# Background work on VectorE pinned in emission order, with larger costs per step, in a hybrid mLSTM and sparse attention block

## The chip, the cores and the metric

The kernel runs on one core of a Trainium2 chip. The metric is the device time of one execution in microseconds (us); three runs give the time of the kernel before, and one more execution was recorded by the hardware profiler.

## What is computed

A decoder block over 512 tokens of width 1024, in float32. One input projection feeds two groups of heads: an mLSTM with four heads behind a short causal convolution, and an attention with eight heads in which each token keeps the 128 best keys by an indexer's score. Both are gated, one output projection joins them, and a gated per-layer embedding and a final norm follow. Cut to what matters here:

```python
def block(x, p, ...):
    u = rmsnorm(x, norm_in)
    m_q, m_k, m_v, m_o, m_z, m_if, a_q, a_k, a_v, a_z, ix_q, ix_k, ix_w = split(u @ w_in)
    mq, mk = split(silu(causal_dwconv(concat(m_q, m_k), conv_w)))      # four taps
    log_i, log_f = m_if[:, :4] + b, log_sigmoid(m_if[:, 4:] + b)
    hm = sigmoid(m_o) * rmsnorm(mlstm(mq, mk, m_v, log_i, log_f)) * m_norm * silu(m_z)
    score = sum_h ix_w[h] * relu(ix_q[h] @ ix_k.T)                      # causal
    sel = top_k(score, 128)
    ha = softmax(a_q @ a_k.T / 8 + rel_bias, over sel) @ a_v * silu(a_z)
    h = x + concat(hm, ha) @ w_out
    h = h + (p @ w_ple) * sigmoid(h @ w_ple_gate)
    return rmsnorm(h, norm_final)
```

## The kernel before

Tokens are cut into four blocks of 128, channels into tiles of 128. Each operand of a product is split into a high and a low part (wh and wl for weights, uH and uL for the normed input), and each product is three matmuls (L212 to L214, or L232 to L234). Weights come in pieces of 128 x 1024; ScalarE rounds a piece to wh (L148), and wl = raw - wh is computed on GpSimd for the even pieces from 8 to 34 and on VectorE for the others (both L149).

TensorE runs the products one after the other: the indexer's queries, mq, mk (with the score matmuls is_ps, L506, put between them), mv in two passes of four PSUM banks, then the gates o and z, the mLSTM woven with further gates, av and aqk, the attention woven with aqk, az and the first output products, the output projection wo, and the embedding. The four banks of a dense product come free when its evacuation is done: for mk two copies on ScalarE (L462, L463), for mv a copy on ScalarE (L545, high part) and a subtraction on VectorE (L546, low part), for each of four token blocks. The evacuations carry a high priority. The score matmuls and the small products of the mLSTM use four other PSUM banks in turn.

Work that no product needs at once is background work: generators in the list `back`, `scores()` (relu on ScalarE, L509, and a weighted sum on VectorE, L514), `sequences()` (the gate scans, L479 to L494), eight `conv()` (three taps on VectorE, L450, a Tanh on ScalarE, L452, and a final step on VectorE, L453), and `topk()` (48 rounds, each a MAX, L524, and a MATCH_REPLACE, L525); later `split_mix()` (L595, L596) is added. `beat()` is called once in each group of dense matmuls and gives one unit of credit; it takes steps of the first generator while the credit isn't negative, and each step's cost (COST_SC, COST_CV, COST_TK, COST_MX, line 33) is taken off. This decides where the instructions are emitted. The final order of each engine's queue is set by a tile scheduler behind that, which moves an instruction ahead or back by its own view of readiness and priority unless it is pinned: `tc.keep_in_program_order` places an instruction behind the one traced just before it on its engine. Queues are in order: an instruction that waits holds all behind it. The bias table of the attention is loaded by a DMA that ScalarE's queue issues (`load_bias`, L440), and it waits for the write of `tdram` (L436).

Of the kernel before, what the change touches and what calls it, by code (L numbers as in the profile page):

```python
# [14 lines left out]
AF = mybir.ActivationFunctionType  # L15
OP = mybir.AluOpType
# [4 lines left out]
S = 512  # L21
# [8 lines left out]
DPLE = 256  # L30
EPS = 1e-6
NTMP, NKEEP = 8, 37
COST_SC, COST_CV, COST_TK, COST_MX, RATE = 1.3, 1.5, 1.5, 3.0, 1.4
NR, NW, ND, NS = 3, 4, 4, 1
QK0 = 10
POOLP = range(8, 36, 2)
# [11 lines left out]
def block_kernel(ctx: ExitStack, tc: tile.TileContext, x, p, w_in, b_gate, conv_w, w_out, norm_in,  # L48
                 m_norm, rel_bias, w_ple, w_ple_gate, norm_final, buckets, out):
    nc = tc.nc  # L50
    V, A, G, T = nc.vector, nc.scalar, nc.gpsimd, nc.tensor
# [30 lines left out]
    def col(name, n=1, bufs=1):  # L82
        return cp.tile([P, n], F32, tag=name, bufs=bufs, name=name)
# [30 lines left out]
    def cw(j, c):  # L114
        return vcols[:, 16 + 8 * j + c:17 + 8 * j + c]
# [52 lines left out]
        return ready.pop(k)  # L168

    back, credit = [], [0.0]  # L170

    def beat():

        credit[0] += 1.0
        while back and credit[0] >= 0.0:
            cost = next(back[0], None)
            if cost is None:
                back.pop(0)
            else:
                credit[0] -= cost  # L180
        if not back:
            credit[0] = 0.0
# [264 lines left out]
    def conv(c, raw):  # L447
        y = mqk[c]
        for j in range(1, 4):
            V.scalar_tensor_tensor(y[:, j:], raw[:, 0:S - j], cw(3 - j, c), y[:, j:], op0=OP.mult, op1=OP.add)  # L450
        yield COST_CV
        A.activation(raw, y, AF.Tanh, scale=0.5)  # L452
        V.scalar_tensor_tensor(y, raw, 1.0, y, op0=OP.add, op1=OP.mult)  # L453
        yield COST_CV

    def evac_qk(c0):
        def go(b, ps):
            c = c0 + b
            y = mqk[c] = keep(f"mqk{c}")
            raw = keep(f"raw{c}")  # L460
            with urgent():
                A.activation(raw, ps, AF.Copy)  # L462
                A.activation(y, ps, AF.Copy, scale=cw(3, c))  # L463
            back.insert(len(back) - 1, conv(c, raw))
        return go
# [3 lines left out]
    fr = [r[96:108, :] for r in rw]  # L469
    lr = [r[64:76, :] for r in rw]  # L470
# [5 lines left out]
    def sequences():  # L476
        A.activation(fr[1], fr[0], AF.Abs)
        A.activation(fr[2], fr[1], AF.Exp, scale=-1.0)
        A.activation(fr[1], fr[2], AF.Ln, bias=1.0)  # L479
        yield 1.0  # L480
        V.scalar_tensor_tensor(lr[2], fr[0], 0.0, fr[1], op0=OP.min, op1=OP.subtract)
        V.tensor_tensor_scan(lr[1], lr[2], lr[0], 0.0, op0=OP.add, op1=OP.max)
        yield 1.0

        arow = sp.tile([P, SW], F32, tag="sL", bufs=1, name="arow")
        ar = arow[64:76]
        for j in range(NT):
            n = S - j * P
            seg = ar[:, OFF[j]:OFF[j] + n]
            V.tensor_tensor_scan(seg, ones[64:76, :].to_broadcast([12, n]), lr[2][:, j * P:], 0.0, op0=OP.mult, op1=OP.add)  # L490
            V.tensor_tensor(lr[3][:, j * P:(j + 1) * P], lr[0][:, j * P:(j + 1) * P], seg[:, 0:P], OP.subtract)
            V.tensor_tensor(seg, seg, lr[1][:, j * P:], OP.subtract)
            yield 1.0
        nc.scalar.dma_start(adram, arow[72:76, 0:1280])  # L494


    sel, ended = {}, [False]
# [22 lines left out]
    def topk():  # L520
        for r in range(TOPK // 8):
            for i in range(1, NT):
                m8 = col(f"m8_{i}", 8, bufs=2)
                V.max(out=m8, in_=sel[i])  # L524
                V.match_replace(out=sel[i], in_to_replace=m8, in_values=sel[i], imm_value=-3e38)  # L525
                yield COST_TK
        for i in range(1, NT):
            V.tensor_scalar(sel[i], sel[i], -2e38, BIG, op0=OP.is_gt, op1=OP.mult)
        ended[0] = True

    back += [scores(), sequences(), topk()]
    run(dense_fm(4, evac_qk(0), name="mq"), dense_fm(4, evac_qk(4), name="mk"))

# [446 lines left out]
```

## Time and profile before

| | us |
|---|---|
| Time, median of three runs | 525.41 (525.35 to 527.21) |
| Profiled execution | 526.94 |
| its span | 524.9 |
| TensorE busy in the span | 498.6 |
| VectorE busy | 349.3 |
| ScalarE busy | 259.8 |
| GpSimd busy | 81.3 |

The span is the recorded stretch of the profiled execution, and all times of rows are counted from its start. A group of instructions is named by its line in the kernel, the engine, and the tiles that it writes and reads. A number in square brackets at the end of a timeline's row is the idle time of the engine ahead of it and what ended that. In the trace, mk runs until 96, pass 0 of mv from 98 to 121, pass 1 from 128 to 152, the first gates until about 198, the mLSTM's stage until about 313 and the attention's until about 400.

### The profile page before, as it was taken

The numbers are of one execution on the slowest core, as the hardware profiler recorded it, in microseconds if no ns is written. First come the engines' busy times: TensorE is split into PE (matmuls) and PEld (weight loads), VectorE is DVE, ScalarE is ACT, GpSimd is POOL, SyncE is SP. The second block draws the span as 40 slices with busy tenths as digits, with TensorE's granted clock in tenths as the row PEclk, the third lists the DMA queues.
The fourth block names the chain that finished last, engine by engine and source line by source line (L and its number), as shares of the span: only waits on it lengthen the run. The fifth ranks groups of instructions, "written<-read, shape, count | busy, mean of one in ns | idle before, by whom it ended". The sixth has DMA issues, their size and how long they took to land.

```text
span 524.9 us, 6706 instructions
## 1 busy us (share of the span) xinstructions
PE 498.6 (95%) x2370; PEld 409.3 (78%) x2370; DVE 349.3 (67%) x718; ACT 259.8 (49%) x518; POOL 81.3 (15%) x110
## 2 busy tenths in 40 slices
PE   4999999894999999999999999999999999999994
PEld 3887878683878888888888787888878888888884
DVE  0945287999999827355745759979887441452744
ACT  5636183763132425465545658767875321232533
POOL 4501022231111322310101012111111000000011
PEclk9999999997999999999999999999999999999998
DMA  8352557322223224223422312121123443213012
GB/s 264 108 181 84 104 87 172 117 82 81 81 85 116 82 81 140 77 92 112 131 81 90 102 61 76 46 81 74 47 82 121 161 160 113 88 41 120 1 51 109
DMA packets 37280, 52.24 MB, mean 100 GB/s; under 512 B 4156, under 2 KB 16732, under 8 KB 37248
## 3 DMA queue, kind: packets, MB, share of 16 engines
q1 hardware_dynamic: 30464, 42.34, 25.2%
q10 hardware_dynamic: 6688, 9.46, 7.3%
q8 instruction: 18, 0.29, 0.2%
q14 instruction: 14, 0.11, 0.1%
q0 software_dynamic: 96, 0.02, 0.0%
HBM read 48.13 MB, written 3.69 MB: 99 GB/s over the span
## 4 chain that ended last, share of the span: by engine, by line
PE 74%; DVE 12%; DMA 8%; ACT 2%; issue 2%; SPq 0%; POOL 0%; POOLq 0%; ACTq 0%; DVEq 0%
DMA tdram<-tv 7%; PE wo L233 4%; PE wo L232 4%; PE wo L234 4%; PE o L212 3%; PE z L212 3%; PE z L214 3%; PE o L213 3%; PE z L213 3%; PE o L214 3%; DVE mqk L450 2%; PE aqk L212 2%; PE aqk L213 2%; PE aqk L214 2%; PE mv L232 2%
## 5 line engine op out<-in xcount | busy, mean ns | idle before, releaser
L148 ACT ACTIVATE wh<-raw 128x1024 fp32r<-128x1024 f32 x70 | 74.0, 1058 | 110.6 <-PE wo L234 36.5
L149 DVE TENSOR_TENSOR wl<-raw,wh 128x1024 fp32r<-128x1024 f32 x56 | 68.6, 1225 | 68.5 <-ACT wh L148 68.3
L149 POOL TENSOR_TENSOR wl<-raw,wh 128x1024 fp32r<-128x1024 f32 x14 | 33.8, 2415 | 134.8 <-ACT wh L148 123.4
L232 PE MATMUL wo<-wh,mixH 128*128 128x512 f32 x96 | 38.9, 405 | 0.1
L234 PE MATMUL wo<-wh,mixL 128*128 128x512 f32 x96 | 37.9, 395 | 0.0
L233 PE MATMUL wo<-wl,mixH 128*128 128x512 f32 x96 | 37.9, 395 | 0.0
L232 PE MATMUL mv<-wh,uH 128*128 128x512 f32 x64 | 26.2, 410 | 8.5 <-DVE v L546 6.6
L212 PE MATMUL aqk<-uH,wh 128*128 128x512 f32 x64 | 26.4, 413 | 0.0
L234 PE MATMUL mv<-wh,uL 128*128 128x512 f32 x64 | 26.0, 406 | 0.0
L525 DVE MATCH_REPLACE8 sc<-m,sc 128x256 f32<-128x256 f32 (+2 forms) x48 | 25.8, 544 | 0.0
L212 PE MATMUL o<-uH,wh 128*128 128x512 f32 x64 | 25.8, 402 | 0.0
L212 PE MATMUL z<-uH,wh 128*128 128x512 f32 x64 | 25.7, 402 | 0.0
L233 PE MATMUL mv<-wl,uH 128*128 128x512 f32 x64 | 25.7, 401 | 0.0
L214 PE MATMUL aqk<-uH,wl 128*128 128x512 f32 x64 | 25.4, 397 | 0.0
L214 PE MATMUL z<-uH,wl 128*128 128x512 f32 x64 | 25.4, 396 | 0.0
L213 PE MATMUL o<-uL,wh 128*128 128x512 f32 x64 | 25.4, 396 | 0.0
L214 PE MATMUL o<-uH,wl 128*128 128x512 f32 x64 | 25.3, 396 | 0.0
L213 PE MATMUL z<-uL,wh 128*128 128x512 f32 x64 | 25.3, 396 | 0.0
L213 PE MATMUL aqk<-uL,wh 128*128 128x512 f32 x64 | 25.3, 395 | 0.0
L524 DVE MAX8 m<-sc 128x8 f32<-128x256 f32 (+2 forms) x48 | 24.8, 550 | 0.2 <-POOL sc L516 0.2
L731 POOL TENSOR_SCALAR bm<-sc,tz 128x128 f32<-128x128 f32 (+1 forms) x16 | 13.7, 857 | 71.3 <-DVE ha L772 21.2
L514 DVE SCALAR_TENSOR_TENSOR sc<-relu,iwt,sc 128x256 f32<-128x256 f32 (+2 forms) x21 | 14.2, 676 | 13.7 <-ACT relu L509 12.9
(245 smaller groups left out, 1363.6 us busy)
## 6 DMA issues: line engine op xcount, KB each, us to landing
raw<-in_w_in_dram SPq DMA_DIRECT2D x44, 512.0 KB, 3.4
raw<-in_w_out_dram SPq DMA_DIRECT2D x12, 512.0 KB, 3.5
raw<-in_w_in_dram SPq DMA_DIRECT2D x16, 256.0 KB, 2.9
raw<-in_w_ple_gate_dram SPq DMA_DIRECT2D x8, 512.0 KB, 3.5
x<-in_x_dram SPq DMA_DIRECT2D x8, 256.0 KB, 5.7
xr<-in_x_dram ACTq DMA_DIRECT2D x2, 1024.0 KB, 5.6
tdram<-tv ACTq DMA_DIRECT2D x1, 1536.0 KB
tz<-tdram ACTq DMA_DIRECT2D x1, 1024.0 KB, 6.3
```

The source lines that it names most:

```text
L148: A.activation(h, raw, AF.Copy)
L149: (G if k in POOLP else V).tensor_tensor(l, raw, f(h), OP.subtract)
L212: T.matmul(banks[b][:, 0:nt], h[:, k, bs], uH[:, kt, tok0:], start=(kt == 0), stop=False)
L213: T.matmul(banks[b][:, 0:nt], h[:, k, bs], uL[:, kt, tok0:], start=False, stop=False)
L214: T.matmul(banks[b][:, 0:nt], l[:, k, bs], uH[:, kt, tok0:], start=False, stop=(kt == KT - 1))
L232: T.matmul(banks[i], aH(kt, i), h[:, k, :], start=first, stop=False)
L233: T.matmul(banks[i], aH(kt, i), l[:, k, :], start=False, stop=False)
L234: T.matmul(banks[i], aL(kt, i), h[:, k, :], start=False, stop=last)
L514: V.scalar_tensor_tensor(sc, r, w, sc, op0=OP.mult, op1=OP.add)
L524: V.max(out=m8, in_=sel[i])
L525: V.match_replace(out=sel[i], in_to_replace=m8, in_values=sel[i], imm_value=-3e38)
L731: G.tensor_scalar(bm[:, 0:n - 256], sel[i][:, 0:n - 256], tz[:, h, 0:1], None, op0=OP.add)
```

## The change

The costs of a step of a convolution (1.5 to 1.9) and of a top-k round (1.5 to 1.75) rise, so that fewer of them are emitted per beat. Four kinds of VectorE instructions are pinned behind the instruction traced before them: the taps and the final step of a convolution, the first step of the gate sequences, and the MAX of a top-k round. The Tanh of a convolution is emitted in the same step as its taps, ahead of the yield.

```diff
-COST_SC, COST_CV, COST_TK, COST_MX, RATE = 1.3, 1.5, 1.5, 3.0, 1.4
+COST_SC, COST_CV, COST_TK, COST_MX, RATE = 1.3, 1.9, 1.75, 3.0, 1.4
...
     back, credit = [], [0.0]
+
+    paced = tc.keep_in_program_order
...
         for j in range(1, 4):
-            V.scalar_tensor_tensor(y[:, j:], raw[:, 0:S - j], cw(3 - j, c), y[:, j:], op0=OP.mult, op1=OP.add)
+            paced(V.scalar_tensor_tensor(y[:, j:], raw[:, 0:S - j], cw(3 - j, c), y[:, j:], op0=OP.mult, op1=OP.add))
+        A.activation(raw, y, AF.Tanh, scale=0.5)
         yield COST_CV
-        A.activation(raw, y, AF.Tanh, scale=0.5)
-        V.scalar_tensor_tensor(y, raw, 1.0, y, op0=OP.add, op1=OP.mult)
+        paced(V.scalar_tensor_tensor(y, raw, 1.0, y, op0=OP.add, op1=OP.mult))
         yield COST_CV
...
-        V.scalar_tensor_tensor(lr[2], fr[0], 0.0, fr[1], op0=OP.min, op1=OP.subtract)
+        paced(V.scalar_tensor_tensor(lr[2], fr[0], 0.0, fr[1], op0=OP.min, op1=OP.subtract))
...
-                V.max(out=m8, in_=sel[i])
+                paced(V.max(out=m8, in_=sel[i]))
```

Lines behind 171 have numbers higher by 2 in the changed kernel (L450 is L452, L546 is L548).

VectorE's queue ahead of the first piece of v in pass 0 of mv; mqk7 is the eighth convolution, sc1 to sc3 are the scores under top-k, v1_0_0 is the low part of v, block 0, pass 0. Before:

```order
L450 SCALAR_TENSOR_TENSOR mqk7_881<-raw7_882,vcols_96,mqk7_881 128x509
L525 MATCH_REPLACE sc3_742<-m8_3_1281,sc3_742 128x512
L525 MATCH_REPLACE sc2_592<-m8_2_1305,sc2_592 128x384
L453 SCALAR_TENSOR_TENSOR mqk7_881<-raw7_882,mqk7_881 128x512
L524 MAX m8_3_1320<-sc3_742 128x8
L525 MATCH_REPLACE sc1_468<-m8_1_1335,sc1_468 128x256
L525 MATCH_REPLACE sc3_742<-m8_3_1320,sc3_742 128x512
L546 TENSOR_TENSOR v1_0_0_1027<-mv0_891,v0_0_0_1026 128x2x256
```

And now, at the same piece of v:

```order
L149 TENSOR_TENSOR wl_1075<-raw_941,wh_1074 128x1024
L455 SCALAR_TENSOR_TENSOR mqk0_623<-raw0_624,mqk0_623 128x512
L452 SCALAR_TENSOR_TENSOR mqk3_665<-raw3_666,vcols_96,mqk3_665 128x511
L608 TENSOR_TENSOR qkL0_1363<-mqk0_623,qkH0_1362 128x512
L452 SCALAR_TENSOR_TENSOR mqk3_665<-raw3_666,vcols_96,mqk3_665 128x510
L452 SCALAR_TENSOR_TENSOR mqk3_665<-raw3_666,vcols_96,mqk3_665 128x509
L455 SCALAR_TENSOR_TENSOR mqk3_665<-raw3_666,mqk3_665 128x512
L548 TENSOR_TENSOR v1_0_0_1024<-mv0_891,v0_0_0_1023 128x2x256
```

The last convolution and the top-k steps are no longer ahead of v1_0_0; convolutions 0 and 3 are, and convolution 2 lies between the pieces of v.

ScalarE's queue in the mk stage, around the DMA of the bias table; relu_746 reads is_ps_743, the first score block of the last token block. Before:

```order
L509 ACTIVATE relu_724<-is_ps_721 128x384
L452 ACTIVATE raw0_624<-mqk0_623 128x512
L452 ACTIVATE raw1_634<-mqk1_633 128x512
L509 ACTIVATE relu_746<-is_ps_743 128x512
L440 DMA tz_1263<-tdram_447 128x8x256
L509 ACTIVATE relu_764<-is_ps_761 128x512
```

And now:

```order
L148 ACTIVATE wh_779<-raw_615 128x1024
L148 ACTIVATE wh_827<-raw_683 128x1024
L511 ACTIVATE relu_724<-is_ps_721 128x384
L442 DMA tz_1256<-tdram_447 128x8x256
L511 ACTIVATE relu_746<-is_ps_743 128x512
L511 ACTIVATE relu_764<-is_ps_761 128x512
```

The two Tanh have moved behind mk, and the DMA stands ahead of relu_746.

VectorE's queue in the first blocks of the mLSTM's first head; st leads to hm and to the transpose hp_ps. Before:

```order
L663 SCALAR_TENSOR_TENSOR st_1756<-st_1756,gcol_1249 128x1
L617 SCALAR_TENSOR_TENSOR go0_1403<-hp_ps_1800,vcols_96,go0_1403 128x128
L663 SCALAR_TENSOR_TENSOR st_1792<-st_1792,gcol_1249 128x1
L617 SCALAR_TENSOR_TENSOR go1_1414<-hp_ps_1800,vcols_96,go1_1414 128x128
L617 SCALAR_TENSOR_TENSOR go0_1403<-hp_ps_1841,vcols_96,go0_1403 128x128
L663 SCALAR_TENSOR_TENSOR st_1833<-st_1833,gcol_1249 128x1
L617 SCALAR_TENSOR_TENSOR go1_1414<-hp_ps_1841,vcols_96,go1_1414 128x128
```

And now:

```order
L665 SCALAR_TENSOR_TENSOR st_1732<-st_1732,gcol_1242 128x1
L619 SCALAR_TENSOR_TENSOR go0_1388<-hp_ps_1776,vcols_96,go0_1388 128x128
L665 SCALAR_TENSOR_TENSOR st_1768<-st_1768,gcol_1242 128x1
L619 SCALAR_TENSOR_TENSOR go1_1399<-hp_ps_1776,vcols_96,go1_1399 128x128
L526 MAX m8_2_1787<-sc2_592 128x8
L527 MATCH_REPLACE sc2_592<-m8_2_1787,sc2_592 128x384
L526 MAX m8_3_1796<-sc3_742 128x8
L527 MATCH_REPLACE sc3_742<-m8_3_1796,sc3_742 128x512
L526 MAX m8_3_1934<-sc3_742 128x8
L527 MATCH_REPLACE sc3_742<-m8_3_1934,sc3_742 128x512
L665 SCALAR_TENSOR_TENSOR st_1809<-st_1809,gcol_1242 128x1
L619 SCALAR_TENSOR_TENSOR go0_1388<-hp_ps_1817,vcols_96,go0_1388 128x128
```

Rounds of top-k stand between the chains of two blocks. As a whole, 18 rounds stand ahead of the mLSTM's first step on VectorE (L641) in the new order, and about 30 behind it; in the old one all 48 are ahead of it. Of the eight mix splits (L596) three stand behind the mLSTM's last block in the new order.

## Rows read from the trace of the kernel before

**Rows 1.** Waits of TensorE: engine, line and releaser: us in total, times, longest.

```profile
PE mv L232 <- DVE v L546: 6.6, 1, 6.6
...
PE mv L232 <- ACT mqk L463: 1.9, 2, 1.6
```

**Rows 2.** Timeline of TensorE between mv's passes: start, us, line, out<-in, [idle, releaser].

```profile
121.34 0.40 PE L234 MATMUL mv<-wh,uL 128*128 128x512 f32 x1
128.31 0.79 PE L232 MATMUL mv<-wh,uH 128*128 128x512 f32 x1 [6.57 <-DVE v L546]
...
131.33 0.39 PE L233 MATMUL mv<-wl,uH 128*128 128x512 f32 x1
```

**Rows 3.** Stretches: busy PE, PEld, DVE, ACT, POOL (instructions), PEclk, DMA, GB/s.

```profile
121.60:128.30 6.70, 0.14 (x1) 0.00 (x0) 6.70 (x16) 4.05 (x7) 2.36 (x1) 0.70 0.24 79
...
200.00:237.00 37.00, 37.00 (x187) 31.12 (x185) 18.97 (x33) 19.27 (x42) 9.39 (x14) 1.00 0.31 99
...
314.00:342.00 28.00, 27.35 (x137) 22.29 (x137) 27.29 (x73) 22.22 (x51) 4.41 (x5) 1.00 0.20 58
```

**Rows 4.** Timeline of VectorE from the gate scans to the first piece of v.

```profile
113.97 1.22 DVE L482 TENSOR_TENSOR_SCAN rows<-rows,rows 12x512 f32<-12x512 f32 x1
...
119.83 0.61 DVE L492 TENSOR_TENSOR arow<-arow,rows 12x256 f32<-12x256 f32 x2
...
121.08 1.22 DVE L149 TENSOR_TENSOR wl<-raw,wh 128x1024 fp32r<-128x1024 f32 x1
122.22 0.74 DVE L450 SCALAR_TENSOR_TENSOR mqk<-raw,vcols,mqk 128x510 f32<-128x510 f32 x1
...
127.57 0.68 DVE L546 TENSOR_TENSOR v<-mv,v 128x512 fp32r<-128x512 f32 x1
```

**Rows 5.** Timeline of ScalarE at the end of pass 0 of mv.

```profile
124.25 0.63 ACT L452 ACTIVATE raw<-mqk 128x512 f32<-128x512 f32 x1 [8.18 <-DVE mqk L450]
```

**Rows 6.** Timeline of TensorE around the start of pass 0 of mv.

```profile
91.04 0.39 PE L214 MATMUL mk<-uH,wl 128*128 128x512 f32 x1
...
96.17 0.40 PE L214 MATMUL mk<-uH,wl 128*128 128x512 f32 x1
98.16 0.51 PE L232 MATMUL mv<-wh,uH 128*128 128x512 f32 x1 [1.59 <-ACT mqk L463]
```

**Rows 7.** Timeline of ScalarE in the mk stage.

```profile
80.03 0.59 ACT L509 ACTIVATE relu<-is_ps 128x512 f32<-128x512 f32 x1
87.98 0.41 ACTq L440 DMA_DIRECT2D tz<-tdram  x1
...
94.98 0.64 ACT L452 ACTIVATE raw<-mqk 128x512 f32<-128x512 f32 x1 [2.95 <-DVE mqk L450]
...
96.94 0.59 ACT L462 ACTIVATE raw<-mk 128x512 f32<-128x512 f32 x1
```

**Rows 8.** Timeline of TensorE in the mk stage, a score matmul.

```profile
87.55 0.39 PE L506 MATMUL is_ps<-ik,qi 128*128 128x512 f32 x1
```

**Rows 9.** A weight split of GpSimd, and a tap of VectorE beside it.

```profile
110.98 2.41 POOL L149 TENSOR_TENSOR wl<-raw,wh 128x1024 fp32r<-128x1024 f32 x1 [4.32 <-ACT wh L148]
...
111.14 2.80 DVE L450 SCALAR_TENSOR_TENSOR mqk<-raw,vcols,mqk 128x509 f32<-128x509 f32 x1
```

**Rows 10.** Page, part 5: the two instructions of a top-k round.

```profile
L525 DVE MATCH_REPLACE8 sc<-m,sc 128x256 f32<-128x256 f32 (+2 forms) x48 | 25.8, 544 | 0.0
...
L524 DVE MAX8 m<-sc 128x8 f32<-128x256 f32 (+2 forms) x48 | 24.8, 550 | 0.2 <-POOL sc L516 0.2
```

**Rows 11.** First chain of the mLSTM: VectorE's step, ScalarE's copy, TensorE's transpose.

```profile
213.22 0.21 DVE L663 SCALAR_TENSOR_TENSOR st<-st,gcol 128x1 f32<-128x1 f32 x1
...
214.09 0.47 ACT L666 ACTIVATE hm<-nm_ps,st 128x256 f32<-128x256 f32 x1 [1.63 <-POOL st L664]
...
214.87 0.38 PE L614 MATMUL hp_ps<-ident,hm 128*128 128x128 f32 x2
```

**Rows 12.** Timeline of TensorE in the attention, a matmul of az.

```profile
336.53 0.51 PE L212 MATMUL az<-uH,wh 128*128 128x512 f32 x1 [0.16 <-DVE ak L713]
```

## The prediction

> **What bounds the kernel now.** I read the busy times first, then the waits of TensorE, then the timelines of each engine at the two longest waits. By the table of times TensorE is busy 498.6 of the 524.9 us, VectorE 349.3, so time can be gained almost only where TensorE stands still. Its list of waits, apart from the start of the kernel, has one large entry: 6.6 us in one piece, in front of a matmul of mv, for a piece of v that VectorE writes; another, in two pieces, is 1.9 us for the copy of mk out of PSUM by ScalarE [rows 1]. Both lie around the same stage.
>
> The 6.6 us stand between the two passes of mv. The last matmul of pass 0 starts at 121.34, the first of pass 1 at 128.31 [rows 2]. The granted clock of the gap is 0.70, against 1.00 in stretches where TensorE is fed all the time [rows 3], and the first matmul behind it takes 0.79, twice its 0.40: the restart begins at the lower of the two levels (1.2 GHz in place of 2.4). Pass 1 needs the PSUM bank that the first piece of v leaves, and VectorE frees it with the row of 127.57 [rows 4]. VectorE has no idle time in front of that row: from 113.97 on it does the gate scans, a weight split, two taps and two finals of the last convolutions, and six instructions of top-k. ScalarE shows the same from its side: its copies of v (L545) stand behind a Tanh that waited 8.18 us for a convolution tap and starts at 124.25 [rows 5]. So the evacuation of v is late because background work stands before it in two in-order queues.
>
> **The change part by part.** It adds no instruction and removes none; it moves them. The profiled execution took 526.94 us for a span of 524.9; its own excess over the median, 525.41, is 1.5 us. I make the sum as differences within the profiled execution and apply them to the median.
>
> (a) *The gap between the passes.* In the new order VectorE passes the first piece of v after convolutions 1, 0 and 3 only, with no top-k round before it, and ScalarE passes it after the Tanh of convolution 3. What the gap costs now: the wait of 6.57, shown at 128.31; the distance 121.34 to 128.31 is 6.97, less 0.23 of a normal step is 6.74. From 128.31 seven matmuls take until the eighth at 131.33, 3.02 us, where 7 x 0.233 = 1.63 would do: 1.39 more. Together -8.1 if the wait goes away whole.
>
> (b) *Pass 0 of mv.* The last matmul of mk starts at 96.17; the last of pass 0 at 121.34. 96 matmuls lie between them in 25.17 us; 96 x 0.233 = 22.4. The excess of 2.8 is the wait of 1.59 at 98.16 [rows 6], the other 0.3 of the 1.9 [rows 1], and steps lost beside them. It comes from ScalarE: its queue held the copy of mk bank 0 until 96.94, though the last matmul on that bank starts at 91.04 [rows 6], because a Tanh of L452 stood in front and waited 2.95 us for a tap [rows 7]. In the new order no Tanh stands between the scores and these copies. I take -2.8; the bound on the small side is the named waits, -1.9.
>
> (c) *A new wait in mk.* The Tanh of convolutions 0 and 1 leave ScalarE's stretch before 80, and in the new order the DMA of the bias table (tz) stands ahead of the relu that in the profile runs at 80.03. That DMA issue is held until 87.98, when the write of tdram has landed [rows 7]. With the move the relu of 80.03 starts at about 88.5 and ends near 89.1. The score matmul at 87.55 takes over the PSUM bank that this relu reads (four banks in turn, and it is the fourth score block after this one) [rows 8]. TensorE so waits from 87.55 to about 89.1: +1.6. The bounds are 0 (if the DMA landed earlier) and 2.2.
>
> (d) *What is late next at the first piece of v.* I rebuild VectorE's queue from the row durations. mk ends, with (c), at about 98.0, and the copies of mk follow to 100; by my count the last score is done near 98.7, then come one weight split of 1.22 and three taps of 0.74, to 102, and the gate's first step at 103, when ScalarE's Abs, Exp, a table load and Ln have followed the copies of mk, and 0.7 more for that step; the scans up to the last L492 took 113.97 to 120.44, 6.5 us [rows 4], so they end at about 110.2 (103 + 0.7 + 6.5). Then six taps, three finals, one weight split and one qk split: 10 x 0.66 + 1.14 = 7.7 (1.14 is the distance from the split at 121.08 to the tap at 122.22, 0.08 under its duration; 0.66 is the tap's 0.74 less the same 0.08). So the first piece of v starts at 117.9 and is done at 118.6; with ScalarE's Tanh and copy ahead of it I put it at 119.1. Pass 1 would start at 98.0 + 22.4 = 120.4. That is a margin of 1.3 us, if no instruction is stretched. But the profile shows stretched ones: a tap of 0.74 took 2.80 at 111.14, while GpSimd's weight split ran from 110.98 to 113.39 [rows 4, 9]. GpSimd's splits of the weights of pass 1 follow ScalarE's, by its new order at about 106 and 117.7 (my estimate), where VectorE has the scans and the taps of convolution 3: each collision costs up to 2.1 (2.80 - 0.74). For the taps I take it; for the scans no row decides. With the one collision the first piece of v is done at 121.2, 0.8 late, with both at 123.0 or so, 2.6 late. I take +1.5, near the middle, with the ends 0 and 2.6.
>
> The Trainium skill (SBUF — State Buffer, "Who interferes with whom") says that a VectorE instruction with two SBUF inputs contends with a GpSimd instruction that reads SBUF and that the loser is fully blocked, while one with at most one SBUF input isn't touched. The rows agree: 2.80 against 0.74 us. This rule speaks against the change, since it puts two-input convolutions where one-input top-k steps stood; by it the scans would be blocked as well, and (d) would be +2.6 in place of +1.5.
>
> (e) *Top-k inside the mLSTM.* The 48 rounds took 24.8 + 25.8 us on VectorE [rows 10], 1.05 us each, all ahead of the mLSTM; in the new order about 30 of them, 32 us, come behind its first step, over some 100 us, where VectorE was busy 18.97 of the first 37 [rows 3]. There is room for them. The risk is latency: per block a small step (L663) leads over GpSimd and ScalarE to a transpose (hp_ps) on TensorE. In the first block the step is at 213.22 and the transpose at 214.87, 1.65 later, without a wait; the last link before the transpose, the copy hm on ScalarE, ends at 214.56, so 0.31 us were to spare [rows 11]. In the new order most rounds stand behind the step, in the time in which VectorE was idle. I take +0.5, from 0 to 2.
>
> (f) *Attention.* The mix splits (L596) move back with the credit, three of the eight behind the last mLSTM block. One takes about 0.7, as the piece of v of the same shape does [rows 4]; VectorE is busy 27.29 of 28 us from 314 to 342, and a matmul of az already waits 0.16 us for it at 336.53 [rows 3, 12]. One split now stands ahead of that wait: +0.7; bounds 0 and 2.
>
> The later convolutions, which now lie in pass 1, cost nothing: VectorE's work is the same, and the first reader of their results on TensorE is the mLSTM, past 198. If that cover fails (a weight split late behind them), it shows as a wait of mv or o for L149.
>
> Sum: -8.1 - 2.8 + 1.6 + 1.5 + 0.5 + 0.7 = -6.6. 525.4 - 6.6 = **518.8 us** (the profiled execution would be at 520.3).
>
> **The rivals.**
> R1, slower: the rounds come ahead of L663. With a whole round (1.05, and 0.08 for the load of MATCH_REPLACE) in front, less 0.31 to spare, each of 16 chains is 0.8 late: 16 x 0.8 = 13, in place of (e)'s 0.5: 518.8 + 12.6 = 531.4. It decides from 0.44 us a chain on (7.1 / 16). For it: the 0.31 to spare is less than one instruction of a round [rows 10]. Against it: the written order has the rounds mostly behind the step, and VectorE idles there.
> R2, no change: the first piece of v stays late by 5 to 6 us (ScalarE's Tanh of convolution 3 is late and holds the copies, a collision on each split). Then (a) gives 2 in place of 8.1 and (d) nothing: 518.8 + 6.1 - 1.5 = 523.4. Against it: the top-k steps and the later convolutions have left the queue.
> R3, clean: no collision, no lost chain, splits hidden: 525.4 - 8.1 - 2.8 + 1.6 = 516.1.
> R4, the pins don't give the emission order: each ties an instruction only to the one traced right before it on the engine. The written order shows it (convolution 1 ahead of 0, two MAX ahead of their turn), but also the rounds out of the way; that it leaves the time at 525 I count under R2.
>
> **How the numbers follow.** My forecast 0.60, R3 0.17, R2 (with R4) 0.13, R1 0.06; 0.04 for other losses in the long stages. 0.5% is 2.6 us and about what a measurement of this kernel can tell from no change. Faster than 522.8: forecast and R3, and a little of R2, 0.79; same 0.13; slower than 528.0: 0.08. The range goes from R3 less half a us to R2: 515.6 to 523.4. It holds (d) at its worst (+1.1), (e) and (f) at their worst (+2.8) together, 522.7.
>
> **What would show it.** The wait of mv for v falls under 2.6 us (a, d); no wait of mv for L463 (b); a new wait of is_ps for the relu (L509, now 511) of about 1.6 at 87.6 (c); the taps of convolution 3 stretched to 2.8 beside GpSimd's split (d); the waits of hp_ps under 2 us together (e); az's wait near 0.9 (f). The prediction is wrong if hp_ps waits many times, or if the wait of mv for v stays over 4.

## The result and the profile after

| | median, us | runs | ratio to before, 95% interval |
|---|---|---|---|
| before | 526.64 | 6 | |
| the changed kernel | 528.98 (528.07 to 530.62) | 6 | 1.0054 (1.0031 to 1.0076) |

The changed kernel is slower by 0.5%: the ratio is that of the mean times, 529.23 and 526.39 us. The forecast was a gain of 1.3% (518.8 us), with 523.4 as the upper end of its range. The profiled execution has a span of 527.7, against 524.9.

The waits of TensorE in the changed kernel (engine, line and releaser: us in total, times, longest), which answer to [rows 1]:

```profile
PE mv L234 <- DVE v L548: 3.7, 1, 3.7
PE hp_ps L616 <- ACT hm L668: 3.6, 3, 2.1
...
PE hp_ps L616 <- ACT st L663: 0.7, 1, 0.7
...
PE pt_ps L757 <- DVE sm L737: 0.4, 1, 0.4
```

The wait of mv for mk's copies (1.9) has left the list, that for v has fallen from 6.6 to 3.7, and the transposes of the mLSTM (hp_ps), which waited 0.4 us in all before, now wait 4.3. The list holds no more than that, so the rest of the loss has to be looked for in TensorE's pace. Its timeline around the two passes of mv, beside [rows 2, 6] (start, us, line, out<-in, idle before and its releaser):

```profile
96.47 0.39 PE L216 MATMUL mk<-uH,wl 128*128 128x512 f32 x1
96.70 0.39 PE L234 MATMUL mv<-wh,uH 128*128 128x512 f32 x1
...
118.86 0.40 PE L236 MATMUL mv<-wh,uL 128*128 128x512 f32 x1
122.97 0.79 PE L234 MATMUL mv<-wh,uH 128*128 128x512 f32 x1 [3.71 <-DVE v L548]
...
127.83 0.63 PE L236 MATMUL mv<-wh,uL 128*128 128x512 f32 x1
...
128.65 0.40 PE L235 MATMUL mv<-wl,uH 128*128 128x512 f32 x1
```

Pass 0 now begins at once behind mk and runs through in 22.16 us. But behind a shorter wait the lower clock lasts longer than before: the usual 0.40 comes back only at 128.65, 5.68 us after the restart, where 13 matmuls at the usual distance of 0.233 need 3.03.

Where the time went is read best from the start of the same piece of work in both traces:

| start of | before | after | difference |
|---|---|---|---|
| mk | 69.11 | 69.23 | +0.1 |
| mv, pass 0 | 98.16 | 96.70 | -1.5 |
| last matmul of pass 0 | 121.34 | 118.86 | -2.5 |
| the first work behind mv (gc_ps) | 152.19 | 148.12 | -4.1 |
| the mLSTM's first products (st_ps) | 197.87 | 193.79 | -4.1 |
| av | 256.12 | 257.35 | +1.2 |
| the attention's first logits (lg_ps) | 313.65 | 315.81 | +2.2 |
| wo | 379.32 | 382.06 | +2.7 |

The changed kernel is ahead by 4.1 us when mv ends and loses 6.8 behind that: 5.3 of them in the first two heads of the mLSTM, 0.9 in the later heads, and 0.6 in the attention. In what follows, the lead at a place is how much earlier a kernel's trace reaches it than the trace before.

The longest wait of hp_ps stands at the first block of the second head. ScalarE, VectorE and TensorE there in the changed kernel:

```profile
238.48 0.20 ACT L664 ACTIVATION_READ_ACCUMULATOR junk<-nm_ps 128x1 f32 x1
...
239.31 0.67 DVE L608 TENSOR_TENSOR qkL<-mqk,qkH 128x512 fp32r<-128x512 f32 x1
...
239.97 0.54 DVE L527 MATCH_REPLACE8 sc<-m,sc 128x384 f32<-128x384 f32 x1
240.43 0.20 DVE L665 SCALAR_TENSOR_TENSOR st<-st,gcol 128x1 f32<-128x1 f32 x1
...
243.34 0.44 PE L616 MATMUL hp_ps<-ident,hm 128*128 128x128 f32 x2 [2.06 <-ACT hm L668]
...
244.90 0.63 PE L216 MATMUL z<-uH,wl 128*128 128x512 f32 x1
```

The step L665 could start when ScalarE's sums are done (238.7) and starts at 240.43, behind rounds of top-k and a split for the next head. From 244.90 seven matmuls run at the lower clock (0.63 us in place of 0.40).

### The profile page after: what moved, and what is told of

The parts are those of the page before. It is cut to its first block, busy times and chain, and to the rows that moved or that the text cites. A ratio compares the mean times of both kernels' runs of the same rounds, so it can differ in the third digit from the quotient of the medians.

```text
span 527.7 us, 6715 instructions
## 1 busy us (share of the span) xinstructions
PE 502.5 (95%) x2370; PEld 412.4 (78%) x2370; DVE 353.4 (67%) x718; ACT 260.4 (49%) x518; POOL 80.3 (15%) x110
## 4 chain that ended last, share of the span: by engine, by line
PE 72%; DVE 15%; issue 5%; ACT 3%; DMA 2%; POOL 2%; SPq 1%; POOLq 0%; ACTq 0%
PE wo L235 4%; PE wo L234 4%; PE wo L236 4%; PE mv L234 2%; DVE wl L149 2%; PE mv L236 2%; PE mv L235 2%; PE z L216 2%; PE z L215 2%; PE z L214 2%; DVE sc L527 2%; PE aqk L215 2%; PE aqk L214 2%; PE mq L214 2%; PE aqk L216 2%
## 5 line engine op out<-in xcount | busy, mean ns | idle before, releaser
L516 DVE SCALAR_TENSOR_TENSOR sc<-relu,iwt,sc 128x256 f32<-128x256 f32 (+2 forms) x21 | 16.8, 799 | 16.9 <-ACT relu L511 15.1
L526 DVE MAX8 m<-sc 128x8 f32<-128x256 f32 (+2 forms) x48 | 25.9, 550 | 0.1
```

The lines of the kernel that those rows point to most:

```text
L516: V.scalar_tensor_tensor(sc, r, w, sc, op0=OP.mult, op1=OP.add)
L526: paced(V.max(out=m8, in_=sel[i]))
```

## The experiments

All ratios are to runs of the kernel before on the same chip.

**e1: the rounds of top-k earlier in the queue.** One number of the changed kernel:

```diff
-COST_SC, COST_CV, COST_TK, COST_MX, RATE = 1.3, 1.9, 1.75, 3.0, 1.4
+COST_SC, COST_CV, COST_TK, COST_MX, RATE = 1.3, 1.9, 0.65, 3.0, 1.4
```

> The changed kernel with the cost of a top-k round at 0.65 in place of 1.75, all else kept: 44 of the 48 rounds stand ahead of the mLSTM instead of 18, and the queue up to the first pieces of v is the same. Theory A (the changed kernel loses in the mLSTM because top-k rounds stand ahead of the step that leads to hp_ps): the waits of TensorE at hp_ps fall from 4.3 us to under 1, the slow matmuls after 244.9 are gone, and the time falls by about 5 us, to 523 to 525. Rival B (the waits of hp_ps come from weight splits and qk splits that stand there anyway): the waits stay over 3 us and the time within 1 us of the changed kernel.

530.32 us, ratio 1.0082 (1.0054 to 1.0110): 1.3 us above the changed kernel by the medians, though the two intervals overlap. The forecast of neither theory came; A had a gain of about 5 us. The busy times of a stretch (us, then busy time of PE, PEld, DVE, ACT, POOL; clock, DMA share, GB/s) and the waits of TensorE:

```profile
153.00:185.00 32.00, 32.00 (x139) 25.71 (x138) 30.89 (x81) 10.33 (x13) 7.23 (x3) 1.00 0.34 100
...
PE hp_ps L616 <- ACT hm L668: 2.1, 1, 2.1
PE nm_ps L657 <- ACT sH L644: 1.6, 1, 1.6
PE o L216 <- DVE wl L149: 1.3, 1, 1.3
```

44 rounds stood ahead of the mLSTM in the queue, but VectorE is full from 153 on (30.89 of 32 us), so that they were worked off late: the last round's MAX starts at 215.1, inside the first head, and all that stood behind them, a weight split too, came late there. A place in a queue is not a time. The later heads, which had no rounds, had no such waits: that speaks for theory A, but it isn't settled by this run.

**e2: two weight splits away from GpSimd.** The changed kernel with

```diff
-POOLP = range(8, 36, 2)
+POOLP = [8, 10, 12, 14] + list(range(20, 36, 2))
```

> The changed kernel with the weight splits of pieces 16 and 18 on VectorE instead of GpSimd. Theory A (v is late because these two splits, at 105.0 and 117.8, block a gate scan for 2.3 us and a tap for 2.1): the scan pair falls from 4.30 to 2.0 and the tap pair from 3.52 to 1.4, VectorE gains two splits of 1.2 of which at most one lies ahead of v, so v is 3 us earlier, the wait of mv for v falls from 3.7 to about 0.5, the slow matmuls behind it go, and the time falls by 4 to 6 us. Rival B (VectorE is simply full, and two more splits cost as much as the blocking): the wait of mv stays at 3 us or more.

524.43 us, ratio 0.9947 (0.9927 to 0.9967), 4.5 us under the changed kernel. VectorE's rows of the gate scans, of the taps of convolution 3 and of v, first in the changed kernel:

```profile
103.94 4.30 DVE L492 TENSOR_TENSOR_SCAN arow<-ones,rows 12x512 f32<-12x512 f32 x2
...
117.41 3.52 DVE L452 SCALAR_TENSOR_TENSOR mqk<-raw,vcols,mqk 128x510 f32<-128x510 f32 x2
121.62 0.69 DVE L455 SCALAR_TENSOR_TENSOR mqk<-raw,mqk 128x512 f32<-128x512 f32 x1 [0.69 <-ACT raw L453]
122.23 0.68 DVE L548 TENSOR_TENSOR v<-mv,v 128x512 fp32r<-128x512 f32 x1
```

and GpSimd's splits beside them in the same kernel:

```profile
105.02 2.41 POOL L149 TENSOR_TENSOR wl<-raw,wh 128x1024 fp32r<-128x1024 f32 x1 [6.92 <-ACT wh L148]
...
117.79 2.59 POOL L149 TENSOR_TENSOR wl<-raw,wh 128x1024 fp32r<-128x1024 f32 x1 [6.63 <-ACT wh L148]
```

With the splits on VectorE:

```profile
104.65 2.04 DVE L492 TENSOR_TENSOR_SCAN arow<-ones,rows 12x512 f32<-12x512 f32 x2
...
116.88 1.53 DVE L452 SCALAR_TENSOR_TENSOR mqk<-raw,vcols,mqk 128x510 f32<-128x510 f32 x2
118.33 1.22 DVE L149 TENSOR_TENSOR wl<-raw,wh 128x1024 fp32r<-128x1024 f32 x1
119.46 0.68 DVE L455 SCALAR_TENSOR_TENSOR mqk<-raw,mqk 128x512 f32<-128x512 f32 x1
120.06 1.28 DVE L548 TENSOR_TENSOR v<-mv,v 128x512 fp32r<-128x512 f32 x2
...
120.80 0.50 PE L234 MATMUL mv<-wh,uH 128*128 128x512 f32 x1 [0.83 <-DVE v L548]
```

Each collision cost 2.0 to 2.3 us (4.30 against 2.04, 3.52 against 1.53), and without them v comes 2.2 us earlier although VectorE has the two splits of 1.22 besides. Theory A holds. The wait of 0.83 that stays isn't followed by slow matmuls, so that the lead when mv ends grows from 4.1 to 8.8 us. In the mLSTM the same waits appear as in the changed kernel (hp_ps 3.6 and 0.7), and take 4.7 of it back before the attention, against 6.2 in the changed kernel: behind the same wait of 2.06 no matmul is slow in this trace, where seven were in the other.

**e3: both edits.**

> Both edits together: round cost 0.65 and the splits of pieces 16 and 18 on VectorE. If the two losses are separate, the gains add: 9 to 11 us under the changed kernel, 518 to 520, and faster than the kernel before by over 1%. If the top-k rounds, now dense behind mv, delay the gates or the pieces of v of pass 1, part of it is lost and waits of o or z for VectorE appear.

524.96 us, ratio 0.9966 (0.9947 to 0.9985). The forecast of 518 to 520 failed: the gains don't add, since e1 has none, and the lead of 9.5 us when mv ends is spent on the same three waits as in e1 (nm_ps 1.6, o 1.4, hp_ps 2.8) and on slower matmuls behind them (a granted clock of 0.66 from 215 to 220).

**e4: the pins alone**, with the costs of before (1.5 and 1.5).

> The pins and the moved Tanh with the old costs (1.5 and 1.5). 14 instead of 12 convolution instructions stand ahead of the first piece of v, 25 instead of 18 rounds ahead of the mLSTM. Theory A: v is later by up to 1.3 us, fewer rounds lie ahead of the mLSTM's steps, so the waits of hp_ps fall a little; within 2 us of the changed kernel. Rival B (the costs are what matters): it lies at the time of the kernel before or under it.

531.65 us, ratio 1.0094 (1.0066 to 1.0122), 2.7 us slower than the changed kernel. The waits:

```profile
PE hp_ps L616 <- ACT hm L668: 5.7, 3, 3.5
PE mv L234 <- DVE v L548: 3.9, 1, 3.9
```

v is no better off and hp_ps waits longer. That seven more rounds stand ahead of the mLSTM didn't help. A round takes less credit there, so that more of them fall in a beat; whether this makes the first heads slower wasn't tried by itself.

**e5: only 18 rounds**, so that none is left for the mLSTM.

```diff
-        for r in range(TOPK // 8):
+        for r in range(6):
```

> The changed kernel with only the first 18 of the 48 top-k rounds (30 rounds are left out, so fewer keys are struck from the scores; everything else is computed). All 18 stand ahead of the mLSTM, and the kernel is the same up to there. Theory A (rounds among the mLSTM's steps hold up its first blocks): hp_ps waits 4.3 us in the changed kernel and under 0.5 here, the slow matmuls at 245 go, az waits less, and the time falls by 5.5 to 6.8 us, to about 523. Rival B (the waits come from the weight splits and qk splits that stand in the same places): hp_ps still waits 3 us or more. VectorE busy time falls by 32 us in any case.

This kernel leaves out 30 of the 48 rounds and so keeps other keys; only its time is of use here. 522.59 us, ratio 0.9934 (0.9909 to 0.9960), 6.4 us under the changed kernel. The waits:

```profile
PE mv L234 <- DVE v L548: 3.7, 1, 3.7
...
PE hp_ps L616 <- ACT st L663: 0.4, 1, 0.4
```

Up to the mLSTM nothing has changed (the wait for v is 3.7 as before, the lead 3.6), and from there to the end the lead stays at 3.6. So all of the 6.8 us go with the 30 rounds, as theory A has it; the weight splits and qk splits, which are still there, cost nothing without them (GpSimd's step L666 at the second head takes 0.55 us again). The attention's 0.6 goes too: with fewer rounds in the list the mix splits are emitted early, and az doesn't fall back. VectorE also has 32 us less to do here, so that this run alone doesn't tell a round's place from its work; e11 and e12 do.

**e6: the bias DMA where it is written.** As e2, and

```diff
-        nc.scalar.dma_start(t, bass.AP(tensor=tdram.tensor, offset=tdram.offset + P - 1,
-                                     ap=[[S - 1, P], [P * S, AH], [1, 2 * P]]))
+        paced(nc.scalar.dma_start(t, bass.AP(tensor=tdram.tensor, offset=tdram.offset + P - 1,
+                                     ap=[[S - 1, P], [P * S, AH], [1, 2 * P]])))
```

> The second experiment's kernel (splits of pieces 16 and 18 on VectorE) with the DMA of the bias table pinned on ScalarE's queue where it is written, behind mv, so that no relu waits behind it. If the wait of is_ps (0.9 us at 88) comes from that DMA issue, it is gone; TensorE is then earlier by 1 us at the end of mk, but the first piece of v is not earlier by as much, so that the wait of mv for v grows from 0.8 by 0 to 1 us. Time between the same and 1 us less than the second experiment.

524.79 us, ratio 0.9970 (0.9954 to 0.9985), the same as e2 within the noise. The wait of is_ps is gone, so it came from that DMA. In its place a wait of hp_ps is longer (2.8 in place of 2.1); the gain in mk can't be seen in the time.

**e7: the rounds by plan.** As e6, and

```diff
     def topk():
+        n = 0
...
-                yield COST_TK
+                n += 1
+                yield 0.7 if n < 26 else 12.0 if n == 26 else 1.0
...
     def beat():
+        if hold[0]:
+            return
         credit[0] += 1.0
...
             c = h // 2
+            hold[0] = True
...
                 tail.append((h, i, hm))
+                hold[0] = False
                 yield
```

> The sixth kernel, and the rounds placed by VectorE's idle time: the first 25 rounds cost 0.7 each (they fall between 150 and 185, where VectorE was idle for 16 us), then a pause of 12 beats over the end of the gates, then 1.0 each, and no beat is counted from a head's start in the mLSTM until its first block has gone through. Theory A (the losses in the mLSTM come from rounds ahead of the first block of each head, not from rounds in the mLSTM as such): hp_ps waits under 1 us in all though 21 rounds are still in the mLSTM, no slow matmuls at 240, and the time is 5 us under the second experiment, 518 to 520. Rival B (any round in the mLSTM costs): half of the loss stays, about 522.

519.08 us, ratio 0.9870 (0.9855 to 0.9884). The waits:

```profile
PE mv L236 <- DVE v L552: 0.8, 1, 0.8
PE hp_ps L620 <- ACT hm L673: 0.8, 3, 0.4
...
PE hp_ps L620 <- ACT st L668: 0.3, 1, 0.3
```

The lead is 9.6 us when mv ends, still 8.7 at av and 8.1 at the first logits. 21 rounds are in the mLSTM, and the first two heads, where 12 of them stand, lose under 1 us; of the 0.6 in the later heads e8 shows 0.5 without any round there. Theory A holds, B falls.

**e8: the costs alone**, without pins and with the Tanh where it was.

> The kernel before with only the two costs raised (1.9 and 1.75), no pins, the Tanh where it was. VectorE's order ahead of the first piece of v is as before (32 convolution instructions, 7 MAX), all rounds are ahead of the mLSTM; the mix splits are later. Theory: the waits of mv stay at 6.6 and 1.9, az may wait 0.5 more; time within 1 us of the kernel before. If it were the costs that move the rounds into the mLSTM, hp_ps would wait here as well.

529.53 us, ratio 1.0067 (1.0050 to 1.0084). Slower than expected. The wait for v is longer:

```profile
PE mv L232 <- DVE v L546: 8.3, 1, 8.3
```

Of the 2.2 us between the spans, 1.0 is lost by the end of mv. Then 0.5 goes in the later heads and 0.6 in the attention, though all 48 rounds are ahead of the mLSTM: the mix splits are as late as in the changed kernel (six of the eight behind 312, against two in the kernel before). hp_ps waits 0.7 us here, so it isn't the costs that bring the rounds among the mLSTM's steps; without pins they float ahead. Costs alone and pins alone are both slower than the kernel before, for different reasons: the first lengthens the wait for v, the second makes that of hp_ps.

**e9: the kernel before with e2's edit.**

> The kernel before with the weight splits of pieces 16 and 18 on VectorE instead of GpSimd, nothing else. If moving these splits is a gain by itself, whatever the order: the tap of 2.80 falls to 0.74, the first piece of v comes 1 to 2 us earlier, and the time falls by about 2 us. If the gain of the second experiment needs the changed order (because in the old one VectorE has 32 convolution instructions, seven MAX and two more splits ahead of v): no gain, within 1 us of the kernel before or slower by up to 2.

524.09 us, ratio 0.9952 (0.9933 to 0.9971), 2.5 us under before. The wait for v:

```profile
PE mv L232 <- DVE v L546: 4.6, 1, 4.6
```

One of the two splits blocked VectorE in the old order too, the one at 110.98 beside the tap of 2.80 [rows 9]; the tap takes 0.75 here. The other, at 125.90, ran beside steps of top-k and a piece of v that kept 0.41 to 0.69 us. Moving the splits is a gain by itself; it isn't owed to the change.

**e10: mix splits first.** As e7, with `back.insert(0, split_mix(h))` in place of `back.append(split_mix(h))`.

> The seventh kernel with the mix splits of a head put at the front of the background list when the head ends, not at its end. Six of the eight then stand ahead of the mLSTM's last step. If the 0.6 us that the changed kernels lose at az come from late mix splits, az's two extra waits (pt_ps 0.3 and 0.4) go away, and the time falls by 0.6 us, to 518.5; if these splits hold up the blocks of the heads instead, hp_ps waits more and the time is the same or higher.

526.96 us, ratio 1.0006 (0.9991 to 1.0021), 8 us more than e7. This run answers nothing on the mix splits: the scheduler changed TensorE's own order with it (the products az start 12.7 us behind the first logits, in e7 15.0), and the attention then waits in many places, among them

```profile
PE pt_ps L763 <- DVE pr L750: 2.1, 3, 1.4
...
PE aqk L216 <- DVE az L690: 1.6, 1, 1.6
```

In the other kernels TensorE's order differs from the changed kernel's in a few places only.

**e11 and e12: the hold alone.** Both are e2 with a round's cost of 1.1; e11 has the hold of e7 besides, no early rounds and no pause.

> The second experiment's kernel with a round's cost at 1.1 and no beat counted from a head's start in the mLSTM until its first block has gone through; no pause, no early rounds, bias DMA as it was. 26 rounds stand ahead of the mLSTM, 22 in it. If what counts is that no round stands ahead of a head's first block: hp_ps waits under 1.2 us, and the time is 4 us under the second experiment, 520 to 521. If it was the early placing that gave the seventh kernel's gain: hp_ps waits 3 us or more, 523 to 525.

> As the kernel before it in this list, without the hold: cost 1.1, splits of pieces 16 and 18 on VectorE. 27 rounds ahead of the mLSTM, 21 in it, some of them ahead of a head's first block. If the hold is what counts: hp_ps waits 2 to 4 us here, the time is 2 to 4 us above the held kernel. If the number of rounds ahead of the mLSTM is what counts, both are equal.

The hold means that no background step is emitted from a head's start until its first block has gone through. e11: 519.51 us, ratio 0.9868 (0.9845 to 0.9891). e12: 526.37 us, ratio 0.9996 (0.9979 to 1.0013). With 26 and 27 rounds ahead of the mLSTM they differ by 6.9 us. The second head's first block without the hold, VectorE, GpSimd and ScalarE in turn, and the wait of TensorE:

```profile
239.28 0.68 DVE L527 MATCH_REPLACE8 sc<-m,sc 128x512 f32<-128x512 f32 x1
239.87 0.21 DVE L665 SCALAR_TENSOR_TENSOR st<-st,gcol 128x1 f32<-128x1 f32 x1
240.00 0.69 DVE L530 TENSOR_SCALAR sc<-sc 128x384 f32<-128x384 f32 x2
240.60 0.69 DVE L598 TENSOR_TENSOR mixL<-go,mixH 128x512 fp32r<-128x512 f32 x1
241.20 1.22 DVE L149 TENSOR_TENSOR wl<-raw,wh 128x1024 fp32r<-128x1024 f32 x1
...
240.23 2.60 POOL L666 TENSOR_TENSOR st<-st,neghalf 128x1 f32<-128x1 f32 x1 [11.60 <-DVE st L665]
...
242.86 0.47 ACT L668 ACTIVATE hm<-nm_ps,st 128x256 f32<-128x256 f32 x1 [4.23 <-POOL st L666]
...
PE hp_ps L616 <- ACT hm L668: 6.6, 2, 4.5
```

and with it:

```profile
233.61 0.21 DVE L668 SCALAR_TENSOR_TENSOR st<-st,gcol 128x1 f32<-128x1 f32 x1
...
233.97 0.55 POOL L669 TENSOR_TENSOR st<-st,neghalf 128x1 f32<-128x1 f32 x1 [10.53 <-DVE st L668]
...
PE hp_ps L618 <- ACT hm L671: 0.2, 1, 0.2
```

What decides is not how many rounds are in the mLSTM, but what stands at a head's first block. ScalarE's Squares were done by 238.7 without the hold, and L665 came at 239.87, behind rounds; then GpSimd's power of 128 numbers took 2.60 us in place of 0.55, beside the last steps of top-k, a mix split and a weight split on VectorE. The hold keeps back mix splits as well as rounds, and these two runs don't tell them apart; in e5, where the mix splits are not held and no rounds follow, nothing is lost, so that the rounds are enough to explain it. e11 and e7 agree within their intervals, so e7's early rounds bring nothing that can be measured on top of the hold.

## Why the prediction was wrong

*What bounds the kernel* was read rightly, as was the direction of the queue: the wait for v came from background work ahead of it. The sum failed in the gap between the passes, terms (a) and (d), where it was 5.0 us off, and in (e), top-k in the mLSTM, where it was 5.7 us off; (b) and (c) gave 1.4 more than forecast.

- (b), pass 0 of mv, held: no wait for mk's copies, 22.16 us for the pass and a normal step from mk to mv (0.23). (b) and (c) together gave -2.6 from mk's start to the end of pass 0, for -1.2 expected.
- (c), the new wait in mk, had the right cause (e6 takes it away) and too large a price: the write of tdram landed earlier in this execution and the DMA was issued at 86.59, not 87.98, so that is_ps lost 0.1 us. In e2 it was issued at 87.29, and is_ps lost 0.95.
- (a) and (d), the gap between the passes, failed: -6.6 expected, -1.6 measured. The first piece of v was done at 122.91, and the text had 123.0 for the case that both collisions happen (by its own terms, 119.1 and twice 2.1, it is 123.3). That it comes so near is in part luck: the gate's first step started at 102.08, 0.9 sooner than assumed, and later steps took that back. Both collisions did happen, the one with the scans too, for which the prediction had no row and took the middle. The rule of the Trainium skill (SBUF — State Buffer, "Who interferes with whom"), by which this case was +2.6, holds in these runs: the scans were blocked as the taps were (4.30 against 2.04 without the split). What the Trainium skill says there of instructions with one input holds only outside VectorE's two-port modes, a condition that the prediction left out; nothing in its sum depends on it. The rest is what the text left out: TensorE came 1.3 us sooner than assumed (119.1 for 120.4), since (c) cost nothing, which only made the wait longer; and behind the wait that remained TensorE restarted at the lower clock again. The end of the old restart was counted as a gain in (a), in full, and a new one was left out of (d). It cost 2.65 (5.68 less 3.03), more than before (1.39).
- (e), top-k in the mLSTM, failed most: +0.5 expected, with 2 as the end, +6.2 measured (5.3 and 0.9). R1 was the mechanism, with 0.06 as its chance and a wrong shape: not 16 chains late by 0.8 us each, but the first blocks of three heads late by 0.7 to 2.1, where low parts (sL), the splits of the next head and rounds pile up ahead of L665, and one restart at the lower clock (seven matmuls from 244.9, about 1.4 us). About 0.5 of the 0.9 in the later heads belongs rather to the late mix splits, since e8 loses it without a round in the mLSTM. The step that failed is "most rounds stand behind the step, in the time in which VectorE was idle": that holds for the blocks behind the first one of a head, but the new queue of a head's first block was not counted out instruction by instruction.
- (f), 0.7 expected at az, 0.6 measured between lg_ps and wo, though not at az itself, but in the transposes before it (pt_ps for sm, 0.4). That late mix splits cause it is borne out by the other traces: from the first logits to wo, e2, e6, e7 and e8, with late mix splits, take 66.3 us as the changed kernel does (66.25), and e1, e4, e5, e9 and e12, with early ones, 65.6 to 65.7 as the kernel before does (65.67). No run moves the mix splits alone; e10 could not show it.
- R2 came in part. Its conditions were met: ScalarE's Tanh of convolution 3 came late (at 120.96, after a wait of 3.25) and each split had its collision. The wait for v fell to 3.7, where R2 had 5 to 6, but with the longer restart the gap gave back 1.6 us, near the 2 that R2 gave it. R2 had no loss in the mLSTM. R4 did not decide anything: the pins put the rounds and convolutions where the written order showed them.

By the sum of the stages: +0.1 - 2.6 - 1.6 + 5.3 + 0.9 + 0.6 = +2.7, and the spans differ by 2.8.

The change thus had a gain to give, and lost it in two places that its own lines don't name: at GpSimd's splits beside the new order, and at the heads' first blocks, where the rounds landed. With the two weight splits on VectorE and the hold at each head's first block it runs in 519.1 to 519.5 us, 1.3% under the kernel before, of which 0.5% (e9) can be had without the change.

## What to carry to other kernels

When background work is moved out of the way of one wait, follow it to where it lands, and count out what then stands ahead of the shortest chain there; total idle time says that there is room, not that it is in the right place. Give a chain across three engines a stretch without background work ahead of its first link, rather than fewer pieces of it. And price a remaining wait of TensorE together with the slow matmuls that may follow it: here a wait of 3.7 us was followed by more of them than one of 6.6.

## What was not expected of the hardware

GpSimd can be the one that loses when it meets VectorE: its power of 128 x 1 numbers, 0.55 us as a rule, took 2.00 us in the changed kernel, 2.60 in e12 and 3.14 in e1, beside VectorE instructions that followed each other without a pause, most of them with two inputs in SBUF. In the changed kernel, behind L665 at 240.43:

```profile
240.56 1.21 DVE L149 TENSOR_TENSOR wl<-raw,wh 128x1024 fp32r<-128x1024 f32 x1
241.69 0.68 DVE L608 TENSOR_TENSOR qkL<-mqk,qkH 128x512 fp32r<-128x512 f32 x1
...
240.78 2.00 POOL L666 TENSOR_TENSOR st<-st,neghalf 128x1 f32<-128x1 f32 x1 [11.46 <-DVE st L665]
```

In all three traces it ended 0.4 us after the last VectorE instruction of that run (here 242.78, after 242.37).

And the time at the lower clock after a wait doesn't follow the wait's length: 7 matmuls behind 6.57 us (before), 13 behind 3.71 (the changed kernel), 7 behind 4.6 (e9), none behind 0.83 (e2). Even the same wait of 2.06 in front of the same transpose was followed by seven in the changed kernel and by none in e2. What sets it wasn't tried.
